# Sums of down weight tiles made by accumulating DMAs instead of VectorE, with the block products in another order

## The chip, the cores and the metric

The kernel runs on one core of a Trainium2 chip. The metric is the device time of one execution in microseconds; the time before is the median of three runs.

## The reference

An encoder trunk of two layers on a sequence of 512 tokens with 1024 channels, in float32. Each layer has three branches (a gated linear recurrence, a spatial gate, a windowed attention), a gated merge with an output projection, and then an MLP with a squared ReLU, which the change touches:

```python
for l in range(DEPTH):                       # DEPTH = 2
    ...
    x = x + merged @ w_out[l]
    hn = rms_norm(x, ln2[l])
    x = x + jnp.square(jax.nn.relu(hn @ w_up[l])) @ w_down[l]   # w_up: 1024x4096, w_down: 4096x1024
return rms_norm(x, final_norm)
```

## The kernel before, in words

All matrix products are made in float32 precision from three matmuls on rounded halves: a weight tile of 128x1024 is cast to `wh` by ScalarE (ACT), and VectorE (DVE) writes the rest `wl = raw - wh`. `wh` and `wl` have two buffers each (`WB = 2`). A projection is then 24 matmuls on TensorE (PE) of 128x128 by 128x512: hi by hi, lo by hi, hi by lo. The host lays all weights out as chunks of 128x1024 in the order in which the kernel takes them (`_order_layer`, the tensor `ws`); one chunk is 512 KB. `wload` loads the next chunk into a `wr` tile (two buffers) by a DMA on SP's queue and splits it; `qload` loads the next chunk into a `wq` tile (`NQ = 10` buffers), also on SP's queue, and it is split later by `wsplit`.

The MLP is done in four quarters of 1024 hidden channels (`qd`). A quarter has eight up projections (`f` 0 to 7); behind each one ScalarE takes the squared ReLU, and `left_sums` makes the left operands of the block products. Then `down` adds the quarter's part of the down projection to the eight `acc` tiles. It is a 2x2 block product with seven multiplications instead of eight (Winograd's form of Strassen's scheme). With b11, b12, b21, b22 for the four 512x512 blocks of the quarter's down weights, each in two tiles, the seven products take on their right side

| product | right side | made by |
|---|---|---|
| 1 | b11 | loaded |
| 2 | b21 | loaded |
| 6 | t2 = t1 + b22 | VectorE (L327) |
| 7 | b12 + b22: `raw[2]`, `raw[3]` after L825 | VectorE (L825) |
| 5 | t1 = b11 + b12 | VectorE (L822) |
| 4 | b21 + t2 | VectorE (L340) |
| 3 | b22 | loaded |

The signs are in the left operands and in the `take`s, so all right sides are plain sums. The products run in the order 1, 2, 6, 7, 5, 4, 3. A product is again 24 matmuls, in two halves (`s_` 0 and 1) of 12 matmuls, one for each of its two weight tiles. `product` splits a tile by `wsplit` just before its half; `take` adds a finished product from PSUM to `acc` (VectorE), or copies it there in the first quarter (ScalarE).

The order of the instructions on each engine is made by a scheduler at build time, which simulates the engines and prefers what stands under `hp()` (high priority); each engine and each DMA queue then runs its instructions in that order and waits on semaphores. SP's queue issues the weight loads. POOL's queue issues the loads of `xr` (L792), the stores of `xspill` (L844) and some small loads, and runs a few elementwise instructions.

The tiles of the MLP take the place of tiles of the branches (`end("br")`, `begin("mlp")`), so the first quarter's `wq` loads can start when the merge no longer needs that memory, while the last projections of the merge (`gz`, `y`) still run. The `wr` loads of these last projections stand on SP's queue among the `wq` loads.

Of the kernel before, what the change touches and what calls it, by code (L numbers as in the profile page):

```python
# [5 lines left out]
F32 = mybir.dt.float32  # L6
# [3 lines left out]
ALU = mybir.AluOpType  # L10

P = 128
S = 512
D = 1024
# [4 lines left out]
CW = 1024  # L19
# [13 lines left out]
def trunk(tc, xT, ws, vec, bsb, snk, wst, rope, cmask, amask, ident, out):  # L33
    nc = tc.nc
# [19 lines left out]
    part = {}  # L54
    BANKS = {"m": 3, "a": 1, "c": 2, "s": 2}
    WR, WB, NZ, NCT, NSM, NQ = 2, 2, 3, 4, 4, 10

    def nm(s):
        ctr[0] += 1
        return f"{s}_{ctr[0]}"  # L60

    def T(tag, name, dt=F32):
        where = part["br"] if tag in BRANCH else sb
        return where.tile([P, S], dt, tag=tag, bufs=SLOTS[tag], name=nm(name))
# [17 lines left out]
    def PT(tag, name):  # L82
        return ps.tile([P, S], F32, tag="p_" + tag, bufs=BANKS[tag], name=nm(name))

    hp = tc.high_priority
    cnt = [0]
# [38 lines left out]
            nc.vector.tensor_tensor(lo, raw, hi.bitcast(F32), ALU.subtract)  # L125
        return hi, lo

    def qload():

        i = cnt[0]  # L130
        cnt[0] += 1
        t = part["mlp"].tile([P, CW], F32, tag="wq", bufs=NQ, name=nm("wq"))
        with hp():
            nc.sync.dma_start(t, ws[i])
        return t

    def wsplit(raw):
        hi = sb.tile([P, CW], F32R, tag="wh", bufs=WB, name=nm("wh"))
        nc.scalar.copy(hi, raw)  # L139
        lo = sb.tile([P, CW], F32R, tag="wl", bufs=WB, name=nm("wl"))  # L140
        nc.vector.tensor_tensor(lo, raw, hi.bitcast(F32), ALU.subtract)  # L141
        return hi, lo
# [6 lines left out]
    def proj(xs, name, w=None, koff=0, nk=KT):  # L149

        hi, lo = w if w is not None else wload()
        pt = PT("m", name)
        for k in range(nk):
            c = slice((koff + k) * P, (koff + k + 1) * P)
            mm3(pt, hi[:, c], lo[:, c], xs[k][0], xs[k][1], k == 0, k == nk - 1)
        return pt
# [94 lines left out]
    def left_sums(h, u, nh):  # L251
# [34 lines left out]
        h.update({2: two(v_, 0), 4: two(v_, 1), 5: two(a_, 0), 6: two(a_, 1), 7: two(b_, 0), 3: two(b_, 1)})  # L286
        return h

    def down(qd, raw, hs, acc):
        b11, b12, b22, b21, t1 = raw[0:2], raw[2:4], raw[4:6], raw[6:8], raw[8:10]  # L290
        V = nc.vector
        first = qd == 0

        def product(n, w, pts, start):
            for s_ in range(2):
                with hp():
                    hi, lo = wsplit(w[s_])
                for k2 in range(2):
                    k = 2 * s_ + k2
                    c = slice(k2 * S, (k2 + 1) * S)  # L300
                    xh, xl = hs[k][n]
                    for p in range(2):
                        t = slice(p * P, (p + 1) * P)
                        nc.tensor.matmul(pts[p], xh[:, t], hi[:, c], start=start and k == 0, stop=False, skip_group_check=True)  # L304
                        nc.tensor.matmul(pts[p], xl[:, t], hi[:, c], start=False, stop=False, skip_group_check=True)  # L305
                        nc.tensor.matmul(pts[p], xh[:, t], lo[:, c], start=False, stop=k == 3, skip_group_check=True)  # L306

        def take(t, fl, pt, sign, fresh=False):
            d = acc[t][fl]
            with hp():  # L310
                if fresh:
                    nc.scalar.activation(d, pt, AF.Copy, scale=float(sign))
                else:
                    V.tensor_tensor(d, d, pt, ALU.add if sign > 0 else ALU.subtract)

        pa = [PT("c", "dA") for _ in range(2)]
        product(1, b11, pa, True)
        for p in range(2):
            take(p, 0, pa[p], 1, first)
        pb = [PT("m", "dB") for _ in range(2)]  # L320
        product(2, b21, pb, True)
        for p in range(2):
            take(p, 0, pb[p], 1)
        t2 = b11
        with hp():
            for s_ in range(2):
                V.tensor_tensor(t2[s_], t1[s_], b22[s_], ALU.add)  # L327
        product(6, t2, pa, False)
        for p in range(2):
            take(2 + p, 0, pa[p], 1, first)  # L330
        pc = [PT("m", "dC") for _ in range(2)]
        product(7, b12, pc, True)
        for p in range(2):
            take(2 + p, 1, pc[p], -1, first)
        product(5, t1, pa, False)
        for p in range(2):
            take(2 + p, 1, pa[p], -1)
        with hp():
            for s_ in range(2):
                V.tensor_tensor(b21[s_], b21[s_], t2[s_], ALU.add)  # L340
        product(4, b21, pc, False)
        for p in range(2):
            take(2 + p, 0, pc[p], 1)
        product(3, b22, pa, False)
        for p in range(2):
            take(p, 1, pa[p], -1, first)
# [182 lines left out]
    for k in range(KT):  # L529
        t = T("l", "x")  # L530
# [21 lines left out]
    for l in range(DEPTH):  # L552
# [251 lines left out]
        n1 = norm_begin("ln1" if l + 1 < DEPTH else "fn", l + 1)  # L804
        acc = [(T("l", "acc"), part["mlp"].tile([P, S], F32, tag="acc", bufs=4, name=nm("acc"))) for _ in range(4)]
        for qd in range(4):
            raw, raw_t1, hs, nh = [], [], [], [0]
            for f in range(8):
                pt = proj(n2.xs, f'up{qd}{f}')
                raw.append(qload())  # L810
                u = T("z", "u")
                with hp():
                    nc.scalar.activation(u, pt, AF.Relu)
                    nc.scalar.activation(u, u, AF.Square)
                    if f % 2 == 0:
                        hs.append(left_sums(None, u, nh))
                    else:
                        hs[-1] = left_sums(hs[-1], u, nh)
                if f == 3:
                    for s_ in range(2):  # L820
                        raw_t1.append(part["mlp"].tile([P, CW], F32, tag="wq", bufs=NQ, name=nm("wq")))
                        nc.vector.tensor_tensor(raw_t1[s_], raw[s_], raw[2 + s_], ALU.add)  # L822
                if f == 5:
                    for s_ in range(2):
                        nc.vector.tensor_tensor(raw[2 + s_], raw[2 + s_], raw[4 + s_], ALU.add)  # L825
            raw += raw_t1
            down(qd, raw, hs, acc)
        for t in range(4):
            for fl in range(2):
# [28 lines left out]
def _order_layer(w_in, w_br, w_out, w_up, w_down):  # L858

    res = []  # L860

    def tproj(w, cols):
        res.append(w[:, cols].reshape(KT, P, P).transpose(1, 0, 2).reshape(P, CW))

    def tok(w, c0):
        for i in range(4):
            res.append(w[i * 256:(i + 1) * 256, c0:c0 + 512].reshape(2, P, 512).transpose(1, 0, 2).reshape(P, CW))

    def col(base, i):
        return slice(base + i * P, base + (i + 1) * P)  # L870

    def head(h):
        for base in (A_FF, A_FB, A_Q):
            tproj(w_in, col(base, h))

    qcols = [np.concatenate([np.arange(C_Q + j * 64, C_Q + j * 64 + 64), np.arange(C_Q + (4 + j) * 64, C_Q + (4 + j) * 64 + 64)]) for j in range(4)]
    crows = np.concatenate([q - C_Q for q in qcols])

    def merge(br):
        wb = w_br[br][crows] if br == 2 else w_br[br]  # L880
        for d in range(KT):
            tproj(w_in, col(G_Z + br * D, d))
            if d % 2 == 0:
                res.append(wb[:, d * P:(d + 2) * P].reshape(4, P, 2, P).transpose(1, 2, 0, 3).reshape(P, CW))


    head(0)
    tok(w_in, A_I)
    for i in range(4):
        tproj(w_in, col(B_U, i))  # L890
    tok(w_in, B_V)
    head(1)
    tproj(w_in, col(C_K, 0))
    tproj(w_in, col(C_V, 0))
    for j in range(4):
        tproj(w_in, qcols[j])
    head(2)
    head(3)
    merge(1)
    for i in range(4):  # L900
        tproj(w_in, col(A_G, i))
    merge(2)
    merge(0)
    for d in range(KT):
        tproj(w_out, col(0, d))
    for qd in range(4):


        quads = [(0, 0), (0, 1), (1, 1), (1, 0)]
        for f in range(8):  # L910
            tproj(w_up, col(qd * D, f // 2 + 4 * (f % 2)))
            kh, fh = quads[f // 2]
            r = qd * D + kh * S + (f % 2) * 2 * P
            res.append(w_down[r:r + 2 * P, fh * S:(fh + 1) * S].reshape(2, P, S).transpose(1, 0, 2).reshape(P, CW))
    return res


def _host(x, w_in, ln1, lb_logits, a_norm, w_s, b_s, sink, w_br, w_out, ln2, w_up, w_down, final_norm):
# [3 lines left out]
    for l in range(DEPTH):  # L922
        chunks += _order_layer(w_in[l], w_br[l], w_out[l], w_up[l], w_down[l])
# [53 lines left out]
```

## Time and profile before

| what | value |
|---|---|
| median of 3 runs | 1780.2 us (1779.21 to 1781.82) |
| the profiled execution, its time | 1779.92 us |
| the profiled execution, its span | 1778.1 us |
| TensorE busy | 1728.6 us, 97% |
| VectorE busy | 1251.2 us, 70% |
| ScalarE busy | 947.4 us, 53% |
| GpSimd (POOL) busy | 93.5 us, 5% |
| bytes moved by DMA | 163.64 MB, mean 92 GB/s |
| granted TensorE clock, mean | 0.992 |

All times are microseconds from the start of the span of one profiled execution. A line of the timeline has start, duration, engine, line of the kernel, operation, out<-in, and in brackets the engine's idle time before it with what ended it. PEld is the loading of weights into TensorE, which runs beside its matmuls. A matmul's row is longer (0.39 us) than the distance to the next one (0.23 us), since matmuls are pipelined. SPq and POOLq are the queues on which SP and POOL issue DMAs; "to landing" is the time from the issue of a DMA to its arrival.

### The profile page before, as it was taken

How to read it: one execution, taken by the hardware profiler on the slowest of the kernel's cores; microseconds unless marked ns; L12 is line 12 of the kernel's file. 1: busy time of each engine (PE TensorE's matmuls, PEld its weight loads, DVE VectorE, ACT ScalarE, POOL GpSimd, SP SyncE). 2: the span in 40 equal slices, each digit the busy share in tenths (PEclk: the TensorE clock that was granted, in tenths of full speed). 3: DMA queues.
4: the chain of work that ended last, by engine and by line, in shares of the span. 5: the costliest groups of instructions: out<-in, count | busy, mean ns of one | idle time of the engine just before them, and what ended most of it. 6: DMA issues, size and time to landing. Idle time of an engine off the chain costs nothing.

```text
span 1778.1 us, 21652 instructions
## 1 busy us (share of the span) xinstructions
PE 1728.6 (97%) x8128; PEld 1426.8 (80%) x8128; DVE 1251.2 (70%) x2053; ACT 947.4 (53%) x1568; POOL 93.5 (5%) x105
## 2 busy tenths in 40 slices
PE   7999999999999999999999999999999999999995
PEld 5788888888778887878788877888878788888884
DVE  5678968675655758586867897777655556677675
ACT  3664876543335554546565669675323364645454
POOL 3012000000000000000110210000000000000000
PEclk9999999999999999999999999999999999999997
DMA  4222212222622232232132211122243223141401
GB/s 171 83 83 72 75 57 72 72 89 83 219 95 95 84 118 92 99 119 71 66 113 83 84 60 60 62 69 78 95 183 119 94 73 127 63 142 61 141 12 48
DMA packets 46728, 163.64 MB, mean 92 GB/s; under 512 B 5664, under 2 KB 6176, under 8 KB 46624
## 3 DMA queue, kind: packets, MB, share of 16 engines
q1 hardware_dynamic: 43488, 152.82, 25.4%
q0 software_dynamic: 2560, 8.39, 1.4%
q8 instruction: 64, 1.05, 0.2%
q10 hardware_dynamic: 576, 1.05, 0.2%
q14 instruction: 40, 0.33, 0.1%
HBM read 158.05 MB, written 4.19 MB: 91 GB/s over the span
## 4 chain that ended last, share of the span: by engine, by line
PE 85%; DVE 7%; ACT 5%; issue 1%; DMA 1%; SPq 0%; POOL 0%; DVEq 0%; ACTq 0%
PE up L145 7%; PE up L146 7%; PE up L147 7%; PE gz L145 5%; PE gz L147 5%; PE gz L146 5%; PE dA L304 3%; PE dA L306 3%; PE dA L305 3%; PE at L422 3%; PE y L145 2%; PE y L147 2%; PE y L146 2%; PE dC L304 2%; PE po L749 2%; PE wo L147 2%
## 5 line engine op out<-in xcount | busy, mean ns | idle before, releaser
L123 ACT CAST wh<-wr 128x1024 fp32r<-128x1024 f32 x220 | 229.7, 1049 | 362.4 <-PE up L146 104.9
L125 DVE TENSOR_TENSOR wl<-wr,wh 128x1024 fp32r<-128x1024 f32 x220 | 269.0, 1224 | 188.0 <-ACT wh L123 178.1
L145 PE MATMUL up<-xh,wh 128*128 128x512 f32 x512 | 199.7, 390 | 0.1
L147 PE MATMUL up<-xh,wl 128*128 128x512 f32 x512 | 199.4, 389 | 0.0
L146 PE MATMUL up<-xl,wh 128*128 128x512 f32 x512 | 199.3, 389 | 0.0
L139 ACT CAST wh<-wq 128x1024 fp32r<-128x1024 f32 x112 | 117.5, 1049 | 152.0 <-PE dA L305 44.1
L141 DVE TENSOR_TENSOR wl<-wq,wh 128x1024 fp32r<-128x1024 f32 x112 | 136.4, 1221 | 49.4 <-ACT wh L139 49.1
L145 PE MATMUL gz<-xh,wh 128*128 128x512 f32 x384 | 152.6, 397 | 2.7 <-ACT wh L123 2.2
L147 PE MATMUL gz<-xh,wl 128*128 128x512 f32 x384 | 151.5, 395 | 1.6 <-DVE wl L125 1.5
L146 PE MATMUL gz<-xl,wh 128*128 128x512 f32 x384 | 151.5, 395 | 0.0
L145 PEld LDWEIGHTS up<-xh,wh 128*128 128x128 f32 x512 | 96.1, 188 | 21.6 <-ACT wh L123 1.7
L147 PEld LDWEIGHTS up<-xh,wl 128*128 128x128 f32 x512 | 96.1, 188 | 19.9
L146 PEld LDWEIGHTS up<-xl,wh 128*128 128x128 f32 x512 | 96.1, 188 | 19.9
L145 PEld LDWEIGHTS gz<-xh,wh 128*128 128x128 f32 x384 | 72.5, 189 | 18.2 <-ACT wh L123 4.1
L147 PEld LDWEIGHTS gz<-xh,wl 128*128 128x128 f32 x384 | 72.5, 189 | 17.4 <-DVE wl L125 3.2
L464 DVE TENSOR_TENSOR ex<-ex 128x256 f32<-128x256 f32 x224 | 85.6, 422 | 0.2
L146 PEld LDWEIGHTS gz<-xl,wh 128*128 128x128 f32 x384 | 72.5, 189 | 13.6
L304 PE MATMUL dA<-wh,sh 128*128 128x512 f32 x208 | 81.9, 394 | 0.5
L305 PE MATMUL dA<-wh,sh 128*128 128x512 f32 x208 | 81.1, 390 | 0.0
L145 PE MATMUL y<-yh,wh 128*128 128x512 f32 x192 | 75.4, 395 | 3.4 <-DVE z L575 1.8
L147 PE MATMUL y<-yh,wl 128*128 128x512 f32 x192 | 75.9, 396 | 0.0
L146 PE MATMUL y<-yl,wh 128*128 128x512 f32 x192 | 75.4, 392 | 0.0
(312 smaller groups left out, 3987.2 us busy)
## 6 DMA issues: line engine op xcount, KB each, us to landing
wr<-in_ws_dram SPq DMA_DIRECT2D x220, 512.0 KB, 3.2
wq<-in_ws_dram SPq DMA_DIRECT2D x64, 512.0 KB, 3.3
x<-in_xT_dram SPq DMA_DIRECT2D x8, 256.0 KB, 9.1
xr<-in_xT_dram POOLq DMA_DIRECT2D x8, 256.0 KB, 4.0
xspill<-xr POOLq DMA_DIRECT2D x8, 256.0 KB, 2.8
xr<-xspill POOLq DMA_DIRECT2D x8, 256.0 KB, 3.0
out_dram<-xf SPq DMA_DIRECT2D x4, 256.0 KB, 2.4
out_dram<-xf ACTq DMA_DIRECT2D x4, 256.0 KB, 2.3
```

Source lines behind the costliest of these rows:

```text
L123: nc.scalar.copy(hi, raw)
L125: nc.vector.tensor_tensor(lo, raw, hi.bitcast(F32), ALU.subtract)
L139: nc.scalar.copy(hi, raw)
L141: nc.vector.tensor_tensor(lo, raw, hi.bitcast(F32), ALU.subtract)
L145: nc.tensor.matmul(pt, whi, xhi, start=first, stop=False)
L146: nc.tensor.matmul(pt, whi, xlo, start=False, stop=False)
L147: nc.tensor.matmul(pt, wlo, xhi, start=False, stop=last)
L304: nc.tensor.matmul(pts[p], xh[:, t], hi[:, c], start=start and k == 0, stop=False, skip_group_check=True)
L305: nc.tensor.matmul(pts[p], xl[:, t], hi[:, c], start=False, stop=False, skip_group_check=True)
L306: nc.tensor.matmul(pts[p], xh[:, t], lo[:, c], start=False, stop=k == 3, skip_group_check=True)
L422: nc.tensor.matmul(pt[:, c], kk(st), qq[:, c], start=True, stop=True)
L464: nc.vector.tensor_tensor(ap_of(ex, o_, d), ap_of(ex, o_, d), ap_of(ex, i_, z), ALU.add)
```

## The change

A DMA issued from POOL can add what it loads to what stands in its destination (`accum_op=ALU.add`). All eight adds of a quarter become such DMAs. They add a block from DRAM to a tile, so a block that is needed in several sums is read from DRAM again for each: a quarter now has ten loads on SP's queue (b11, b21, t, t1, b22, two tiles each; b22 is loaded once as the start of `t` and once by itself) and eight accumulating DMAs on POOL's queue. `t` goes through three states in one place: b22 + b12 for product 7, then + b11 for product 6, then + b21 for product 4; the last two additions (`further`) come between the products and wait until the product before has split the tile. The ten loads and the first four sums are recorded together at the first up projection of the quarter instead of one load at each up projection. Product 7 now comes before product 6: the order is 1, 2, 7, 6, 5, 4, 3.

```diff
-    def qload():
-
-        i = cnt[0]
-        cnt[0] += 1
+    def qload(i, *more):
+
         t = part["mlp"].tile([P, CW], F32, tag="wq", bufs=NQ, name=nm("wq"))
         with hp():
             nc.sync.dma_start(t, ws[i])
+            for j in more:
+                wadd(t, j)
         return t
+
+    def wadd(t, j):
+        nc.gpsimd.dma_start(t, ws[j], accum_op=ALU.add)
...
+    def down_loads(i):
+
+        c11, c21, c12, c22 = [(i + 2 * q, i + 2 * q + 1) for q in range(4)]
+        b11 = [qload(j) for j in c11]
+        b21 = [qload(j) for j in c21]
+        t3 = [qload(j, k) for j, k in zip(c22, c12)]
+        t1 = [qload(j, k) for j, k in zip(c11, c12)]
+        b22 = [qload(j) for j in c22]
+        return b11, b21, t3, t1, b22, c11, c21
+
     def down(qd, raw, hs, acc):
-        b11, b12, b22, b21, t1 = raw[0:2], raw[2:4], raw[4:6], raw[6:8], raw[8:10]
+        b11, b21, t, t1, b22, c11, c21 = raw
         V = nc.vector
         first = qd == 0
+
+        def further(cs):
+            with hp():
+                for s_ in range(2):
+                    wadd(t[s_], cs[s_])
...
         product(2, b21, pb, True)
         for p in range(2):
             take(p, 0, pb[p], 1)
-        t2 = b11
-        with hp():
-            for s_ in range(2):
-                V.tensor_tensor(t2[s_], t1[s_], b22[s_], ALU.add)
-        product(6, t2, pa, False)
+        pc = [PT("m", "dC") for _ in range(2)]
+        product(7, t, pc, True)
+        further(c11)
+        for p in range(2):
+            take(2 + p, 1, pc[p], -1, first)
+        product(6, t, pa, False)
+        further(c21)
         for p in range(2):
             take(2 + p, 0, pa[p], 1, first)
-        pc = [PT("m", "dC") for _ in range(2)]
-        product(7, b12, pc, True)
-        for p in range(2):
-            take(2 + p, 1, pc[p], -1, first)
         product(5, t1, pa, False)
         for p in range(2):
             take(2 + p, 1, pa[p], -1)
-        with hp():
-            for s_ in range(2):
-                V.tensor_tensor(b21[s_], b21[s_], t2[s_], ALU.add)
-        product(4, b21, pc, False)
+        product(4, t, pc, False)
...
         for qd in range(4):
-            raw, raw_t1, hs, nh = [], [], [], [0]
+            hs, nh = [], [0]
+            base = cnt[0] + 8
             for f in range(8):
                 pt = proj(n2.xs, f'up{qd}{f}')
-                raw.append(qload())
+                if f == 0:
+                    raw = down_loads(base)
...
-                if f == 3:
-                    for s_ in range(2):
-                        raw_t1.append(part["mlp"].tile([P, CW], F32, tag="wq", bufs=NQ, name=nm("wq")))
-                        nc.vector.tensor_tensor(raw_t1[s_], raw[s_], raw[2 + s_], ALU.add)
-                if f == 5:
-                    for s_ in range(2):
-                        nc.vector.tensor_tensor(raw[2 + s_], raw[2 + s_], raw[4 + s_], ALU.add)
-            raw += raw_t1
+            cnt[0] += 8
             down(qd, raw, hs, acc)
```

The host's order of the chunks follows: in a quarter the eight up chunks come first and then the blocks b11, b21, b12, b22, two chunks each. In the order that the scheduler gives, the ten `wq` loads of a quarter stand together on SP's queue: in the merge of layer 0 before the `wr` load that stood behind the first four, in layer 1 where eight stood together, and in the later quarters behind the second `wr` load of the quarter's up projections. On POOL's queue the first four sums of a layer alternate with the last `xr` loads. PE has as many instructions as before, and outside the quarters the order on PE and ACT is almost the same.

More of the change, by code (lines that the diff above doesn't have):

```diff
@@ L906, in _order_layer @@
     for qd in range(4):
-        quads = [(0, 0), (0, 1), (1, 1), (1, 0)]
         for f in range(8):
             tproj(w_up, col(qd * D, f // 2 + 4 * (f % 2)))
-            kh, fh = quads[f // 2]
-            r = qd * D + kh * S + (f % 2) * 2 * P
-            res.append(w_down[r:r + 2 * P, fh * S:(fh + 1) * S].reshape(2, P, S).transpose(1, 0, 2).reshape(P, CW))
+        for kh, fh in ((0, 0), (1, 0), (0, 1), (1, 1)):
+            for i in range(2):
+                r = qd * D + kh * S + i * 2 * P
+                res.append(w_down[r:r + 2 * P, fh * S:(fh + 1) * S].reshape(2, P, S).transpose(1, 0, 2).reshape(P, CW))
     return res
```

## The prediction

> **What bounds the kernel now.** I read the page's table of engines first.
>
> ```profile
> span 1778.1 us, 21652 instructions
> PE 1728.6 (97%) x8128; PEld 1426.8 (80%) x8128; DVE 1251.2 (70%) x2053; ACT 947.4 (53%) x1568; POOL 93.5 (5%) x105
> ```
>
> The profiled execution took 1779.92 us, 1.8 us outside its span of 1778.1, and lies 0.3 us under the median of 1780.2; the sum below is made against 1779.9. TensorE is busy nearly throughout, but the share is an average, so the next view is the table of windows, cut to the stretches where the changed code runs: the four quarters of the MLP in layer 0 and in layer 1.
>
> ```profile
> 544.50:871.00 326.50, 326.13 (x1427) 265.68 (x1426) 224.54 (x291) 169.59 (x228) 1.15 (x1) 1.00 0.27 89
> 1388.00:1714.00 326.00, 325.77 (x1427) 266.23 (x1427) 216.69 (x285) 165.88 (x227) 1.14 (x1) 1.00 0.29 96
> ```
>
> The columns are length, PE, PEld, DVE, ACT and POOL busy, granted clock, DMA share, GB/s. PE is busy 326.13 of 326.5 us and 325.77 of 326.0 at clock 1.00: TensorE sets the time here, and taking work from VectorE (224.54 us busy) can win at most the missing 0.4 + 0.2 us. What the change can do inside the quarters is to open gaps. To see how much room there is, I read the timeline of one half product (12 matmuls), in the steady rhythm near the end of a quarter:
>
> ```profile
> 860.76 1.05 ACT L139 CAST wh<-wq 128x1024 fp32r<-128x1024 f32 x1 [1.71 <-PE dC L305]
> 860.79 0.39 PE L304 MATMUL dA<-wh,sh 128*128 128x512 f32 x1
> 861.84 1.22 DVE L141 TENSOR_TENSOR wl<-wq,wh 128x1024 fp32r<-128x1024 f32 x1 [0.16 <-ACT wh L139]
> 863.49 1.05 ACT L139 CAST wh<-wq 128x1024 fp32r<-128x1024 f32 x1 [1.68 <-PE dA L305]
> 863.51 0.39 PE L304 MATMUL dA<-wh,sh 128*128 128x512 f32 x1
> 864.42 0.62 PE L306 MATMUL dA<-wl,sh 128*128 128x512 f32 x2
> ```
>
> A half product takes 863.51 - 860.79 = 2.72 us on PE, a product 5.44. The two `wh` buffers make a tile's cast start when the half before last ends: the cast at 860.76 serves the half that starts at 863.51, and its `wl` is finished at 861.84 + 1.22 = 863.06.
>
> **Part 1: the adds leave VectorE.**
>
> ```profile
> L822 DVE TENSOR_TENSOR wq<-wq,wq x16: 1216/1224/1227, 459.2 to 1653.6; 128x1024 f32<-128x1024 f32 x16
> L825 DVE TENSOR_TENSOR wq<-wq,wq x16: 1216/1218/1226, 463.2 to 1662.8; 128x1024 f32<-128x1024 f32 x16
> L327 DVE TENSOR_TENSOR wq<-wq,wq x16: 1217/1218/1219, 586.2 to 1713.3; 128x1024 f32<-128x1024 f32 x16
> L340 DVE TENSOR_TENSOR wq<-wq,wq x16: 1211/1216/1219, 595.8 to 1722.7; 128x1024 f32<-128x1024 f32 x16
> ```
>
> 64 adds of 1.22 us are 78 us of VectorE. Inside the quarters they are worth at most 0.6 us by the windows; I take 0. Only the first ones of each layer (from 459.2) run outside, in the merge; see part 3. The products keep their number of matmuls, and the `take`s only change places: 0.
>
> **Part 2: product 7 to product 6, in each of 8 quarters.** The tile `t` is split for product 7, then a DMA from POOL adds `c11` to it, then it is split for product 6, which now follows directly. Nothing else lies between, so this is a new wait on PE's path. The room: `wl` of product 7's half is done at 863.06 in the rhythm above. Product 6's same half starts two halves after 863.51, at 868.95, and first reads `wl` 0.91 later (864.42 - 863.51), at 869.86. Before that stand 1.08 from the cast's start to the start of `wl` and 1.22 for `wl`: the sum must have landed by 867.56. That leaves 4.5 us. The second half has the same room, and a late first half moves it along, so a delay counts once a quarter. If the sum is late, ACT and DVE stand at the split of product 6 with the `take`s of product 7 behind it; PE then has nothing else queued.
>
> No accumulating DMA is in the trace. Nearest rows, from the DMA views (of the whole run, of 350 to 360 us, of one quiet and one full stretch) and the timeline:
>
> ```profile
> wq<-in_ws_dram SPq DMA_DIRECT2D x64, 512.0 KB, 3.3
> xr<-in_xT_dram POOLq DMA_DIRECT2D x3, 256.0 KB, 3.4
> DMA to landing us min/median/max: 2.9/3.6/6.0
> wq<-in_ws_dram SPq DMA_DIRECT2D x1, 512.0 KB, 9.0
> 460.00:468.00 8.00, 8.00 (x37) 6.62 (x36) 8.00 (x11) 2.51 (x3) 1.07 (x2) 1.00 0.97 378
> 462.04 0.68 DVE L178 TENSOR_TENSOR mgl<-mg,mgh 128x512 fp32r<-128x512 f32 x1
> 463.02 0.54 POOL L792 DMA_DIRECT2D xr<-in_xT_dram  x1 [12.42 <-DVE mgl L178]
> ```
>
> POOL issues 0.3 us after the VectorE instruction that it waits for (462.72 to 463.02). From below, issue to landing is bounded by 3.3 us, what 512 KB take from SP; from above by 9.0, a 512 KB load behind other loads. I take 5.5, an estimate: 3.4 us for 256 KB from POOL, 0.7 for the other 256 KB at the 378 GB/s of the full stretch, 1.4 because the old 512 KB must be read as well. This is nearer to the lower end since few other loads run in this stretch. So 0.3 + 5.5 - 4.5 = 1.3 us a quarter, **+10.4 us** for eight; the ends are 0 (0.3 + 3.3 is under 4.5) and 4.8 a quarter, 38.4.
>
> The Trainium skill, Collectives: The Full Stack, section "The bandwidth ceiling: the fold count and why AG ≠ RS ≠ AR", says that an adding transfer runs at half a copy's rate, not because of the add but because it reads two sources. By a copy's price (3.4 + 0.7) the sum would be 0 for this part; with the second read it is the value taken. No run shows it yet.
>
> The sum for product 4 (`c21`) has product 5 in between, 5.44 us more room, so 9.9: 0 at 5.8, and 0 still at 9.3. POOL does next to nothing in a quarter (1.15 us), so its queue costs nothing there.
>
> **Part 3: loads in another order, at the merge of each layer.** Each quarter now issues 10 loads from SP together instead of 8 spread over the up projections, and 8 accumulates. The bytes (18 x 512 KB for 8 x) lift 89 GB/s by 64, far under 378: 0 inside the quarters. SP takes its queue in order, so the third `wr` of the next quarter waits behind the `b22` loads, which wait for product 3's splits. These end 2.3 us into product 3's first half; with three loads left at 1.4 us each the `wr` lands about 7 us into product 3, and its cast comes 10.9 us in: 0. In layer 0 the ten loads stand ahead of the merge's `wr`:
>
> ```profile
> 451.21 2.15 SPq L134 DMA_DIRECT2D wq<-in_ws_dram  x4
> 456.94 0.33 SPq L121 DMA_DIRECT2D wr<-in_ws_dram  x1
> 462.17 1.05 ACT L123 CAST wh<-wr 128x1024 fp32r<-128x1024 f32 x1 [0.54 <-PE y L146]
> 466.11 1.22 DVE L125 TENSOR_TENSOR wl<-wr,wh 128x1024 fp32r<-128x1024 f32 x1
> 467.60 0.40 PE L147 MATMUL gz<-xh,wl 128*128 128x512 f32 x1
> ```
>
> Four went first; now ten: a 512 KB load takes 1.4 us of transfer at 378 GB/s, so 1.9 of its 3.3 is start, and 451.21 + 1.9 + 11 x 1.4 = 468.5 is the landing of that `wr`. With cast and `wl` it is 470.8, and PE wants it at 467.60: 3.2 us, up to 7 if the first sums and the `xr` loads share the engines. I take **+4**. In layer 1:
>
> ```profile
> 1310.05 4.23 SPq L134 DMA_DIRECT2D wq<-in_ws_dram  x8
> 1320.77 0.47 PE L145 MATMUL y<-yh,wh 128*128 128x512 f32 x1 [1.47 <-DVE gz L611]
> 1322.95 0.80 PE L147 MATMUL gz<-xh,wl 128*128 128x512 f32 x1 [1.48 <-DVE wl L125]
> 1330.86 1.03 ACT L123 CAST wh<-wr 128x1024 fp32r<-128x1024 f32 x1
> 1318.19 1.23 DVE L822 TENSOR_TENSOR wq<-wq,wq 128x1024 f32<-128x1024 f32 x1 [1.78 <-DMA wq<-in_ws_dram]
> ```
>
> Here eight were together already, and VectorE stood 1.78 us at an add for its load, with `gz` and `wl` behind it: PE's gaps of 1.47 and 1.48 go with the adds, -2.95. What is late next is the `wr` behind ten loads: 1310.05 + 1.9 + 11 x 1.4 = 1327.4, wanted at 1330.86 - 2.95 = 1327.9 by its cast; with sums between, 1 us late, up to 2.2. I take **-2**. The first sums also stand between the `xr` loads on POOL, which are needed from 510 us on,
>
> ```profile
> L796 DVE SCALAR_TENSOR_TENSOR xr<-wo,xr x16: 690/692/692, 510.0 to 1417.9; 128x512 f32<-128x512 f32 x16
> ```
>
> some 35 us later: 0. Sum: 10.4 + 4 - 2 = +12.4, so 1779.9 + 12.4 = **1792 us**.
>
> **The rivals.** *The sums are covered.* If an accumulate lands within 4.2 us, only the merge counts: 1779.9 + 4 - 2 = 1782, and 1777 if the ten loads don't hold PE up either. This is the case on the other side, not slower than before. For it speaks that 256 KB from POOL come down in 2.9; against, that the tile is twice as large and is read too. It decides at 4.2 us from issue to landing. Chance 0.28.
>
> *The accumulate is slow*, over 7 us, because POOL has more to write per row or the add itself has a rate of its own. The nearest row is the 9.0: 2.8 to 4.8 us a quarter, so 1804 to 1820, more if even product 4's sum comes late (beyond 9.6). For it: nothing in the trace shows the operation's rate; against: the plain rows are all far lower when the queues are quiet. Chance 0.22.
>
> *VectorE holds up POOL's issue.* A POOL issue that waits for the end of a VectorE instruction loses up to 1.22 us; eight times that is 10, 1802. The row at 463.02 speaks against: its issue took the usual 0.54 us among VectorE adds. Chance 0.05. The Trainium skill, SBUF — State Buffer, section "Who interferes with whom", says that VectorE's two-port modes shut GpSimd out of descriptor writing, and that tensor_tensor has no such mode; the 0.54 us agrees.
>
> **How the numbers follow.** My forecast, landing in 4.2 to 7 us, has 0.45 and reaches from 1782 to 1804. The range goes from 1779 (the covered case with little lost at the merge) to 1822 (the slow one at 9.0), which leaves out a rare gain and the still slower sums. A measurement tells some 0.2% from no change, 3.6 us. Slower by more: 0.43 of the forecast's 0.45, 0.22 and 0.05, 0.70. The same: 0.02 and most of the covered case, 0.26. Faster needs both merges to go well at once: 0.04.
>
> **What would show it.** Right: in each quarter one PE gap, or two, of 1 to 2 us at the first matmuls of product 6, with ACT's cast before them released by the DMA onto `wq`; in the DMA issues a POOL row of 512 KB near 5.5 us; a gap of some 4 us at the layer 0 merge released by ACT `wh` L123; none behind the adds in layer 1. Wrong: PE busy over 326 us in both windows again (covered), or gaps of 3 us and more a quarter and a landing of 7 and more (slow), or gaps at the up projections, which would mean that SP's order costs inside the quarters.

## The result and the profile after

| | before | after |
|---|---|---|
| median of 4 runs each, us | 1780.38 (1779.21 to 1781.82) | 1806.11 (1804.07 to 1808.03) |
| profiled execution, us (span) | 1779.92 (1778.1) | 1805.59 (1803.8) |

The ratio is 1.0144, 95% interval [1.0126, 1.0162]: 25.7 us slower. The forecast was 1792, 11.8 slower: the direction was right, but the kernel lost about twice as much. The head of the page of after, with its DMA queues (packets, MB, share of 16 engines) and the chain that ended last:

```profile
span 1803.8 us, 21788 instructions
PE 1737.3 (96%) x8128; PEld 1427.6 (79%) x8128; DVE 1185.0 (66%) x1989; ACT 945.3 (52%) x1568; POOL 148.4 (8%) x169
q1 hardware_dynamic: 45792, 161.21, 25.8%
q0 software_dynamic: 11776, 41.95, 11.7%
PE 59%; issue 21%; DVE 7%; DMA 6%; ACT 5%; POOL 0%; SPq 0%; DVEq 0%; ACTq 0%; POOLq 0%
```

VectorE lost 66 us of work, 1251.2 to 1185.0, and the time rose. The total names no place, so the next step is to cut the span at points that both kernels have: PE's start of one `gz` run in the merge of layer 0 (the one behind 0.61 us of idle time), of the first up projection of each layer, of the first `f` of layer 1, and of the last column sums. Before, then after, from the timelines of PE:

```profile
456.57 0.50 PE L145 MATMUL gz<-xh,wh 128*128 128x512 f32 x1 [0.61 <-ACT wh L123]
544.63 0.39 PE L145 MATMUL up<-xh,wh 128*128 128x512 f32 x1
878.49 0.48 PE L145 MATMUL f<-xh,wh 128*128 128x512 f32 x1
1417.75 0.39 PE L145 MATMUL up<-xh,wh 128*128 128x512 f32 x1
1760.54 0.77 PE L188 MATMUL cs<-ones_t,sqa 128*128 128x1 f32 x3 [3.99 <-DVE sqa L234]
```

```profile
454.57 0.50 PE L148 MATMUL gz<-xh,wh 128*128 128x512 f32 x1 [0.61 <-ACT wh L123]
552.39 0.39 PE L148 MATMUL up<-xh,wh 128*128 128x512 f32 x1
892.47 0.48 PE L148 MATMUL f<-xh,wh 128*128 128x512 f32 x1
1437.39 0.39 PE L148 MATMUL up<-xh,wh 128*128 128x512 f32 x1
1785.81 0.34 PE L191 MATMUL cs<-ones_t,sqa 128*128 128x1 f32 x1 [3.54 <-DVE sqa L237]
```

The differences of neighbouring starts are four stretches. For the kernels tried later they are read in the same way; all in us:

| kernel | merge, layer 0 | quarters, layer 0 | to layer 1's quarters | quarters, layer 1 |
|---|---|---|---|---|
| before | 88.06 | 333.86 | 539.26 | 342.79 |
| after | 97.82 | 340.08 | 544.92 | 348.42 |
| first sums left out | 96.92 | 340.97 | 540.96 | 348.72 |
| late start | 95.60 | 343.03 | 541.61 | 351.45 |
| 7 before 2 | 98.05 | 332.63 | 546.08 | 342.55 |
| before, no adds | 96.75 | 331.04 | 540.63 | 339.95 |
| spread, 7 before 2 | 88.06 | 333.10 | 534.39 | 342.34 |
| before, spread | 88.06 | 333.91 | 534.42 | 342.72 |
| spread | 88.05 | 339.68 | 534.40 | 347.30 |
| plain | 96.97 | 332.67 | 542.87 | 341.78 |

After against before: +9.76, +6.22, +5.66, +5.63, together 27.3; 2.0 less before the first point (the start, where the kernels do the same work, differs by some 4 us among the executions of this study) and 0.4 more behind the last make the 25.7. So the quarters cost 11.85 and the merges 15.4. The last column also holds PE's wait for the last column sums, which is no part of the quarters: 3.99 us in before, 3.54 in after, and 2.67 to 4.00 among all ten kernels. Without it the quarters of layer 1 cost 6.08 and all quarters 12.3.

**The quarters.** The first product 6 of layer 0, from the timelines of VectorE, POOL, ACT and PE of after:

```profile
606.08 1.23 DVE L144 TENSOR_TENSOR wl<-wq,wh 128x1024 fp32r<-128x1024 f32 x1 [1.46 <-ACT wh L142]
607.61 0.91 POOL L138 DMA_DIRECT2D wq<-in_ws_dram  x1 [43.89 <-DVE wl L144]
613.24 1.04 ACT L142 CAST wh<-wq 128x1024 fp32r<-128x1024 f32 x1 [4.43 <-DMA wq<-in_ws_dram]
614.34 0.51 PE L322 MATMUL dA<-wh,sh 128*128 128x512 f32 x1 [0.90 <-ACT wh L142]
```

Read it as a chain: the split of product 7 ends at 607.31, POOL issues 0.30 later, ACT starts its cast 5.63 after the issue with the DMA as its releaser, PE starts 1.10 after that, having stood 0.90. This is the wait that the prediction drew, link by link. The same sums of the other quarters land 5.2 to 5.6 us after their issue. The DMA view of after has the operation's price over all 64, with the first sums of each quarter, which run beside other loads:

```profile
wq<-in_ws_dram POOLq DMA_DIRECT2D x64, 512.0 KB, 6.1
DMA to landing us min/median/max: 5.2/6.1/18.5
```

**The merges.** SP's queue, ACT and PE at the merge of layer 0, then the windows around it (length, PE, PEld, DVE, ACT, POOL, granted clock, DMA share, GB/s):

```profile
449.22 6.92 SPq L132 DMA_DIRECT2D wq<-in_ws_dram  x10
457.11 16.70 SPq L121 DMA_DIRECT2D wr<-in_ws_dram  x3
471.15 1.04 ACT L123 CAST wh<-wr 128x1024 fp32r<-128x1024 f32 x1 [4.44 <-DMA wr<-in_ws_dram]
472.25 0.79 PE L148 MATMUL gz<-xh,wh 128*128 128x512 f32 x1 [6.92 <-ACT wh L123]
```

```profile
457.00:465.00 8.00, 8.00 (x37) 6.57 (x35) 3.95 (x7) 1.24 (x2) 4.74 (x7) 1.00 1.03 402
465.00:473.00 8.00, 1.07 (x4) 0.50 (x2) 2.85 (x4) 2.19 (x3) 0.56 (x1) 0.84 1.06 295
471.00:475.00 4.00, 2.71 (x6) 1.71 (x7) 1.83 (x2) 1.96 (x3) 0.55 (x1) 0.50 1.06 266
475.00:479.00 4.00, 4.00 (x15) 3.18 (x14) 1.22 (x1) 0.65 (x1) 0.00 (x0) 0.72 1.05 281
```

Ten `wq` loads go in one row, the `wr` that PE needs is issued 8 us after the row's start, and its cast waits for it until 471.15; PE stands 6.92 us. The DMA engines are full from 457 on (shares of 1.03 to 1.06), but while the sums run they are counted with only 295 GB/s, against 402 just before. The rows behind the gap show something more: the granted clock is 0.50 and 0.72 when PE works again. The stretch is 9.76 us longer and the gap only 6.92 of it; the other 2.84 is matmuls at half clock. In layer 1 the gap is

```profile
1349.14 0.79 PE L148 MATMUL gz<-xh,wh 128*128 128x512 f32 x1 [7.74 <-ACT wh L123]
```

### The profile page after: what moved, and what is told of

Same layout as the page of the kernel before. It is cut to its first block, busy times and chain, and to the rows that moved or that the text cites. A ratio compares the mean times of both kernels' runs of the same rounds, so it can differ in the third digit from the quotient of the medians.

```text
span 1803.8 us, 21788 instructions
## 1 busy us (share of the span) xinstructions
PE 1737.3 (96%) x8128; PEld 1427.6 (79%) x8128; DVE 1185.0 (66%) x1989; ACT 945.3 (52%) x1568; POOL 148.4 (8%) x169
## 3 DMA queue, kind: packets, MB, share of 16 engines
q0 software_dynamic: 11776, 41.95, 11.7%
## 4 chain that ended last, share of the span: by engine, by line
PE 59%; issue 21%; DVE 7%; DMA 6%; ACT 5%; POOL 0%; SPq 0%; DVEq 0%; ACTq 0%; POOLq 0%
PE gz L148 4%; PE gz L149 4%; PE gz L150 4%; DMA wq<-in_ws_dram 3%; PE up L150 3%; PE up L148 3%; PE up L149 3%; PE at L435 3%; PE dA L324 2%; DMA wr<-in_ws_dram 2%; PE dA L322 2%; PE dA L323 2%; PE y L148 2%; PE y L150 2%; PE y L149 2%
## 5 line engine op out<-in xcount | busy, mean ns | idle before, releaser
L138 POOL DMA_DIRECT2D wq<-in_ws_dram x64 | 57.0, 893 | 585.3 <-DVE wl L144 496.3
```

What stands on the lines that cost most here:

```text
L138: nc.gpsimd.dma_start(t, ws[j], accum_op=ALU.add)
```

## The experiments

Two theories for the merges, the open part. **A**: the first four sums share the DMA engines with `wr` and slow it. **B**: the ten `wq` loads stand in one piece ahead of `wr` in SP's queue, and two `wr` buffers, 2 x 5.44 = 10.9 us of PE's work, don't bridge it. For the quarters the rival to the wait between products 7 and 6 is that the added loads disturb them in another way. Four kernels ran first, four more after them; the second group ran against 1779.11 us for before, the first against 1779.31.

**First sums left out.** The first four sums of each layer's first quarter are left out of the computation; the ten loads stay.

```diff
-        t3 = [qload(j, k) for j, k in zip(c22, c12)]
-        t1 = [qload(j, k) for j, k in zip(c11, c12)]
+        t3 = [qload(j, *((k,) if sums else ())) for j, k in zip(c22, c12)]
+        t1 = [qload(j, *((k,) if sums else ())) for j, k in zip(c11, c12)]
...
-                    raw = down_loads(base)
+                    raw = down_loads(base, qd > 0)
```

> Leaves out the first four sums (b22 + b12 and b11 + b12) of the first quarter of each layer, so those right sides lack b12; the ten loads stay together. Theory A, the sums share the DMA engines with the merge's last wr loads: of the 6.92 and 7.74 us gaps at the merges at most 3.2 and 1 are left, the time falls by 9 to 13 us, to about 1795. Theory B, ten loads ahead on SP's queue are the cause by themselves: the gaps stay at 6 us and more and the time within 3 us of 1806. Both: the gaps at product 6 stay, about 12 us over eight quarters.

Measured: 1802.14 us, ratio 1.013 [1.0115, 1.0145]. PE's gaps at the two merges, from its timeline:

```profile
472.65 0.79 PE L148 MATMUL gz<-xh,wh 128*128 128x512 f32 x1 [5.49 <-ACT wh L123]
1346.85 0.80 PE L148 MATMUL gz<-xh,wh 128*128 128x512 f32 x1 [3.56 <-ACT wh L123]
```

5.49 of 6.92 and 3.56 of 7.74 remain without any sum, and the time lies between what the two theories expected. The burst of loads (B) carries the larger part of the gap in layer 0 and a little under half in layer 1; the sums on the shared engines (A) add 1.4 and 4.2 us.

**Late start.** A one-column copy on VectorE ties all loads of the first quarter to the output projection's fourth step (`xcur[3]`), away from the merge.

```diff
+    GATE = 3
...
+        if gate[0] is not None:
+            nc.vector.tensor_copy(t[:, 0:1], gate[0][:, 0:1])
...
+                    gate[0] = xcur[GATE] if qd == 0 else None
                     raw = down_loads(base)
```

> The first quarter's ten loads and with them its first four sums wait, by a one-column copy on VectorE into each tile, until the fourth tile of the output projection is done, some 50 us later. Theories A and B alike: both merge gaps go, and in layer 1 also the 3 us that the adds cost before, so 1806 - 13.4 - 3 or so, 1790 to 1793. If the time stays above 1800, the merge's 13 us come from something else than the first quarter's transfers.

Measured: 1804.53 us, ratio 1.0146 [1.0131, 1.0161], a miss. By the sign named above, a time over 1800 would speak against the first quarter's transfers as the cause; the trace shows that the gap moved with them. SP and PE:

```profile
521.73 6.77 SPq L137 DMA_DIRECT2D wq<-in_ws_dram  x8
529.50 3.05 SPq L122 DMA_DIRECT2D wr<-in_ws_dram  x2
548.31 0.80 PE L153 MATMUL up<-xh,wh 128*128 128x512 f32 x1 [7.40 <-ACT wh L124]
```

Eight of the ten loads stand in one row. The merge's gap is gone, and a gap of 7.40 us stands at the first up projection, 19 us after that row of `wr` issues; in layer 1 it is 6.97 us, at the same place. The burst costs about the same in both places: the output projection also takes one `wr` every 5.44 us. So the merge is no special place, and B must be read as any burst ahead of any `wr`.

**7 before 2.** Products in the order 1, 7, 2, 6, 5, 4, 3, so that product 2 lies between product 7 and product 6. Product 2's PSUM tiles come from another group of banks (`s` for `m`).

```diff
-        pb = [PT("m", "dB") for _ in range(2)]
-        product(2, b21, pb, True)
-        for p in range(2):
-            take(p, 0, pb[p], 1)
         pc = [PT("m", "dC") for _ in range(2)]
         product(7, t, pc, True)
         further(c11)
...
+        pb = [PT("s", "dB") for _ in range(2)]
+        product(2, b21, pb, True)
+        for p in range(2):
+            take(p, 0, pb[p], 1)
         product(6, t, pa, False)
```

> Only the order changes again: 1, 7, 2, 6, 5, 4, 3, so that product 2 (5.44 us) lies between product 7 and product 6. Theory A, each quarter loses what the sum's landing (5.5 to 6.1 us) and POOL's 0.3 exceed the room of 4.5: the room becomes 9.9, the gaps at product 6 go, and the time falls by 10 to 12 us to about 1795. Rival C, the quarters lose because the extra transfers disturb the weight loads or TensorE all over: no gap moves and the time stays within 3 us of 1806.

Measured: 1795.39 us, ratio 1.0093 [1.0076, 1.011], as expected. No gap is left at the start of product 6, and the quarters take 332.63 and 342.55, 7.45 and 5.87 less than in after. The `c11` sums land as before, 5.2 to 5.7 us after their issue; the median of all 64 rises to 7.2 because the first sums of the quarters take longer. So the wait that follows from product 7 standing right before product 6 is what the quarters lost. The merges keep their gaps, 7.61 and 9.93 us; why the second is 2.2 us longer than in after was not followed up.

**Before, no adds.** The kernel before with its 64 VectorE adds left out (the products use unsummed tiles): what the change could win on VectorE at best.

```diff
-                V.tensor_tensor(t2[s_], t1[s_], b22[s_], ALU.add)
...
-                V.tensor_tensor(b21[s_], b21[s_], t2[s_], ALU.add)
...
-                        nc.vector.tensor_tensor(raw_t1[s_], raw[s_], raw[2 + s_], ALU.add)
...
-                        nc.vector.tensor_tensor(raw[2 + s_], raw[2 + s_], raw[4 + s_], ALU.add)
+                        raw_t1.append(raw[s_])
```

> The kernel before without its 64 VectorE adds (products 4 to 7 take unsummed blocks). What the relief of VectorE is worth by itself: by the prediction 0.6 us in the quarters and 3 us at the merge of layer 1, so 1776 to 1777. If VectorE had been holding TensorE up in the quarters, it would be 1770 or less.

Measured: 1781.1 us, ratio 1.0012 [1.0003, 1.0022], a miss. The quarters gained 2.82 and 2.84 us, and a new loss at the merges took it back. SP and PE:

```profile
449.29 6.35 SPq L134 DMA_DIRECT2D wq<-in_ws_dram  x10
470.77 0.79 PE L145 MATMUL gz<-xh,wh 128*128 128x512 f32 x1 [5.41 <-ACT wh L123]
1334.62 0.79 PE L145 MATMUL gz<-xh,wh 128*128 128x512 f32 x1 [3.17 <-ACT wh L123]
```

Without the adds the two tiles of t1 are not needed either, so the ten `wq` buffers take eight loads of the first quarter and two of the next, and here too ten loads end up in one row on SP. There is no accumulating DMA in this kernel, and its gaps, 5.41 and 3.17, are near those of the first experiment (5.49 and 3.56): the burst has this price without any sum.

**Spread, and 7 before 2.** The ten loads of the first quarter each wait for another step of the output projection, so that SP's queue alternates `wr` and `wq`; the order of the products as above.

```diff
+        if gate[0]:
+            nc.vector.tensor_copy(t[:, 0:1], gate[0].pop(0)[:, 0:1])
...
+                    gate[0] = xcur[0:8] + xcur[7:8] * 2 if qd == 0 else []
                     raw = down_loads(base)
```

> Both repairs at once: the first quarter's ten loads each wait for another step of the output projection (one a step, so the queue alternates wr and wq), and product 7 stands before product 2. Theory B (the burst starves the two-deep wr prefetch): the gaps of the run with 7 before 2 alone, 7.61 and 9.93 us in the merges, go and do not come back elsewhere; 1795.4 - 17.5 = 1778, so level with before or up to 2 us under it (its two gaps of 1.5 us in layer 1's merge are gone). Theory A (the sums' own share of the DMA engines delays wr, in whatever order): spread sums still slow wr; some 3 to 6 us of gaps stay, 1781 to 1784.

**Before, spread.** The kernel before, VectorE's adds kept, with only its first quarter's eight loads tied one by one to the same steps. The copy in `qload` is that of the late start.

```diff
+                gate[0] = xcur[f] if qd == 0 else None
                 raw.append(qload())
```

> The kernel before, VectorE's adds kept, with only the first quarter's loads tied one by one to the output projection's steps. If the two gaps of 1.47 and 1.48 us in layer 1's merge come from loads or adds of that quarter running early, they go: 1779.8 - 2.95, about 1776.5. If they don't depend on it: the same as before, 1779 to 1780.

**Spread.** The change with the spread loads, its own order of products.

> The change with the spread loads alone, its own order of products. Theory B: the gaps of 6.92 and 7.74 us at the merges go and none takes their place: 1806.1 - 14.7 = 1791.4, and the eight gaps at product 6 stay, about 1.07 us and 0.5 us each. Theory A: a part of the 14.7 stays, 1795 to 1800.

Measured, with the ratio to before: spread and 7 before 2 1773.55 us, 0.9968 [0.9957, 0.998]; before, spread 1773.98 us, 0.997 [0.9959, 0.9981]; spread alone 1785.22 us, 1.0033 [1.0021, 1.0045]. SP's queue in the first of them:

```profile
517.06 0.33 SPq L136 DMA_DIRECT2D wq<-in_ws_dram  x1
518.27 0.33 SPq L121 DMA_DIRECT2D wr<-in_ws_dram  x1
522.05 0.33 SPq L136 DMA_DIRECT2D wq<-in_ws_dram  x1
523.30 0.33 SPq L121 DMA_DIRECT2D wr<-in_ws_dram  x1
```

In all three the merge of layer 0 takes 88.05 to 88.06 us, as before, and no gap comes back elsewhere. Spread alone keeps the loss of the quarters (339.68 and 347.30), as expected. The same sums over the same DMA engines cost the merges nothing once loads and sums come one at a time: B, with A as an addition to the burst only. One thing stays open in B: in each burst the loads stand ahead of `wr` on its queue and also fill the DMA engines. A burst on another queue was not tried, so the runs don't tell which of the two makes `wr` late. All three came out 2.5 to 6.2 us under what was expected, mostly because the expectation took the gaps off and left the clock in place. Before itself had such a stretch, in layer 1's merge; its PE rows and windows there (PE alone: length, busy, clock, DMA share, GB/s):

```profile
1320.77 0.47 PE L145 MATMUL y<-yh,wh 128*128 128x512 f32 x1 [1.47 <-DVE gz L611]
1322.95 0.80 PE L147 MATMUL gz<-xh,wl 128*128 128x512 f32 x1 [1.48 <-DVE wl L125]
1323.54 0.63 PE L145 MATMUL gz<-xh,wh 128*128 128x512 f32 x1
1323.97 0.63 PE L146 MATMUL gz<-xl,wh 128*128 128x512 f32 x1
```

```profile
1318.00:1322.00 4.00, 1.49 (x5) 1.00 1.03 421
1322.00:1326.00 4.00, 3.05 (x8) 0.57 0.90 316
1326.00:1330.00 4.00, 4.00 (x19) 1.00 0.28 102
```

From 1323.54 to 1325.67 the matmuls start 0.43 us apart instead of 0.227. The spread loads take 4.84 to 4.87 us off this stretch in each of the three kernels: 1.47 + 1.48 of gaps and 1.9 of slow clock. This is the gain over before, and it has nothing to do with the sums: the kernel before with spread loads has all of it. What the change itself adds to that version is 0.81 us in the quarters of layer 0; the 0.38 in layer 1 are less than the difference in the wait for the last column sums (3.28 against 4.00). The medians, 1773.55 and 1773.98, are not distinguishable.

**Plain.** The changed kernel with POOL's 64 DMAs as plain loads onto the same tiles; the adding is left out.

```diff
-        nc.gpsimd.dma_start(t, ws[j], accum_op=ALU.add)
+        nc.gpsimd.dma_start(t, ws[j])
```

> The changed kernel with POOL's 64 DMAs as plain loads of the same tiles onto the same tiles (the adding is left out; same waits, same places, same bytes from DRAM). If the adding is the price (a second read at the destination): plain landing about 3.4 to 4.1 us, issue 0.54 us, the gaps at product 6 go (-10 to -12 us); the merge's burst of ten loads and four more keeps 5 to 7 us of gap in each layer: 1793 to 1796. If POOL's queue itself is slow whatever it does: landing stays 5.2 us and more, and the time 1804 to 1806.

Measured: 1791.18 us, ratio 1.0066 [1.0052, 1.008], 1.8 us under the expected 1793 to 1796. The DMA queue and POOL's line of this kernel, then POOL's line of after:

```profile
q0 software_dynamic: 11776, 41.95, 6.9%
L138 POOL DMA_DIRECT2D wq<-in_ws_dram x64: 530/530/597, 462.0 to 1741.7; - x64
DMA to landing us min/median/max: 3.4/4.0/12.0
```

```profile
L138 POOL DMA_DIRECT2D wq<-in_ws_dram x64: 852/862/1597, 460.3 to 1757.0; - x64
```

Same queue, places and bytes, and the adding alone raises the landing from 3.4 to 5.2 (fastest) and from 4.0 to 6.1 (median), POOL's issue from 0.53 to 0.86. For the `c11` transfers alone it is 3.5 to 3.7 against 5.2 to 5.6. Before's q0 took 1.4% with 8.39 MB; the 64 DMAs are the rest: (6.9 - 1.4)% of 1790.8 is 98 us, 1.54 each on all engines, against (11.7 - 1.4)% of 1803.8, 186 us, 2.90 each. An adding load thus holds the engines 1.9 times as long. The Trainium skill, Collectives: The Full Stack, section "The bandwidth ceiling: the fold count and why AG ≠ RS ≠ AR", has an adding transfer in a ring between cores at half a copy's rate; the 1.9 agrees. With the plain loads the gaps at product 6 are gone, and the merges keep 5.55 and 5.85 us. In layer 0 that is the gap of the ten loads by themselves (5.49); in layer 1 four more plain loads lengthen it by 2.3 us (from 3.56), and the adding by another 1.9 (to 7.74).

## Why the prediction was right in one part and wrong in the other

- **Part 2, product 7 to product 6 (+10.4): right in mechanism, near in size.** Its links, 0.3 + 5.5, were measured as 0.30 and, up to ACT's cast, 5.63. That the 5.5 came so near is in part luck: the plain load lands in 3.5 to 3.7 here, where the forecast's terms make 4.1, and the adding puts 1.8 on top, where it had 1.4. Against the plain loads, and without the wait for the last column sums, the sums cost the quarters 7.41 + 6.43 = 13.84 us, 1.73 a quarter for the 1.3 of the forecast. The forecast counted one delay a quarter; in the three later quarters of each layer idle times stand at both tiles of product 6, up to 0.43 us at the first and 0.06 to 0.35 at the second.
- **Part 1, the adds in the quarters (0, at most 0.6): too small.** Without adds before's quarters are 5.66 us shorter, 0.7 a quarter. The bound was read from PE's busy time, and that column hides short waits. In before's quarter:

```profile
597.95 0.39 PE L305 MATMUL dB<-wh,sh 128*128 128x512 f32 x1
598.40 0.50 PE L304 MATMUL dA<-wh,sh 128*128 128x512 f32 x1
```

  0.45 between two starts for the usual 0.227 is 0.22 lost, but the first record lasts 0.39, so only 0.06 counts as idle. Of these 5.7 us the change kept 1.5 (plain against before, without the wait for the last column sums): 13.84 - 1.54 is the measured 12.3, nearer to 10.4 than 13.84 because two errors partly took each other back. Where the other 4.1 us went was not followed up.
- **Part 3, the merges (+4 and -2, measured +9.76 and +5.66): the step that failed.** The ten loads ahead of `wr` were in the text, but the sum failed in three ways. First, the landing of `wr` behind ten loads, 3.2 us late by the sum: without any sums it left 5.49 of gap in layer 0 and 3.56, for about 0, in layer 1. In layer 0 the `xr` loads are large enough to account for the difference, though no run leaves them out, by the DMA view of 449 to 472 us of the kernel without first sums:

```profile
q0 software_dynamic: 320, 1.05, 14.6%
```

  14.6% of 23 us is 3.4 us of the engines, which the sum had only in its upper end. Layer 1 in the same kernel, on SP, POOL and ACT:

```profile
1325.81 6.69 SPq L132 DMA_DIRECT2D wq<-in_ws_dram  x10
1333.85 0.54 POOL L805 DMA_DIRECT2D xr<-xspill  x1 [9.75 <-DVE mgl L181]
1345.75 1.04 ACT L123 CAST wh<-wr 128x1024 fp32r<-128x1024 f32 x1 [0.30 <-DMA wr<-in_ws_dram]
```

  The cast starts 19.94 us after the row's first issue, where the sum had the landing at 17.35 and the cast wanted at 17.85. To leave no gap it would have had to start 3.56 earlier, at 16.38: the landing was 2.6 us too early in the sum and the want 1.5 too late. The sum had left out a `wr` issued 0.7 us before the row and two `xr` loads; at its own 1.4 us for 512 KB they make 2.8 us, enough for the first of the two, but that is argued and not tested. Second, the sums' own share, taken as 0.8 and 1 us: 1.43 and 4.18, with 2.9 us of all engines for each sum, on average. Third, it priced no gap with the clock: PE comes out of such a gap at half clock, 2.84 us in layer 0 and, with the 4.87 of before's stretch taken off, 5.66 + 4.87 - 7.74 = 2.79 in layer 1. Before's own gaps went as forecast, and with the clock they were worth 4.87, not 2.95. (The forecast's second window, 1388 to 1714, also began 30 us before layer 1's first up projection at 1417.75; the gaps it missed there are none, so no number hangs on it.)
- **The rivals.** The covered case fell: landing 5.2 at the least for the 4.2 at which it decides. The slow accumulate gave a time near the measured one, from another cause: the eight waits for a `c11` sum in the chain last 5.29 to 5.55 us, and the rest came from the merges. VectorE did not hold up POOL's issue of the sums between the products: all 32 came 0.29 to 0.31 us after the end of the last `wl`.
- **The signs named beforehand.** The gaps at product 6 with ACT released by the DMA onto `wq`, and none behind the adds of layer 1, came as said, though the gaps are 0.90 us and less instead of 1 to 2; the gap at layer 0's merge came 7 instead of 4, and one of 7.74 in layer 1 was not named.

A deeper `wr` prefetch would test B from the other side; it was not tried.

## What to carry to other kernels

A queue that serves a shallow prefetch must not get a burst: ten 512 KB loads ahead of loads that come due every 5.44 us cost PE 6.2 to 8.9 us here, slow clock included (against the kernels with spread loads), and 9.8 to 11.7 with adding loads beside them; tied one by one to the steps of the work beside them they cost nothing. An add that moves from an engine to a DMA is not free: it holds the DMA engines 1.9 times as long as a load and puts its 5.2 us and more on the path if its tile is used right before and after. Price a gap on PE with the slow clock behind it, and look for lost time in start-to-start distances, not in the busy share.

## What was not expected of the hardware

The slow clock needs no single long gap. Behind gaps of 3.17 to 9.93 us a stretch grew by 1.8 to 3.4 us more than its gap (9.76 for 6.92, 8.69 for 5.41; in layer 1 against the kernels with spread loads), and it also came behind two gaps of 1.47 and 1.48 us within 4 us (PE worked 1.49 of the 4 us from 1318). The quarters' gaps of 0.9 us kept clock 1.00, and so did this single one in before:

```profile
1101.07 0.50 PE L145 MATMUL y<-yh,wh 128*128 128x512 f32 x1 [1.80 <-DVE z L575]
```

So the length of one gap does not decide alone. The Trainium skill, TensorE: Matmul & The Clock Gate, section "HAM oscillation — how this bites in real kernels", puts the abstract rule at no idle gap of PE over some 3.4 us; the gaps from 3.56 us up agree, and the one of 3.17 and the pair of 1.5 us, all under it, show that the rule as stated is not enough here. The other surprise is a full set of DMA engines at 295 GB/s while sums run, against 402 to 422 with plain loads: full is a share of time, not a rate. The bytes counted for an adding load are those of a plain one (q0 has 41.95 MB in both), so a second read, if there is one, does not show in the rate.
